# Layer 1's prompt attention: two heads' score matmuls issued in turn on the two row halves of the array

## The chip, the cores and the metric

The kernel runs on one core of a Trainium2 chip. The metric is the device time of one execution in microseconds (us). Before the change it was 2068.98 us, the median of 3 runs (2065.84 to 2069.39).

TensorE multiplies: weights are loaded into the array, a second operand streams past them, and the result lands in PSUM, which has 8 banks of 512 fp32 columns. VectorE (DVE) and ScalarE (ACT) read it from there, GpSimd (POOL) works on SBUF alone, and SyncE (SP) issues the DMAs. Each engine runs its own instructions in order and waits on semaphores for the others.

## The reference, cut to what matters

The program is one step of a 2-layer decoder for a prompt of 512 tokens and 8 samples of 8 tokens. What is changed is the prompt's part of layer 1's attention. There are 8 heads of 64 dimensions and three key groups of window and dilation (128, 1), (512, 4) and (2048, 16). Each query attends to distances 0, d, 2d, ... up to its window in each group, and the groups are merged by their softmax denominators:

```
for gi, (window, dilation) in enumerate(((128, 1), (512, 4), (2048, 16))):
    s = einsum(q[gi], k[gi]) * 64 ** -0.5, masked to distances 0, d, ..., window
    m, p = max(s), exp(s - max(s));  den = sum(p);  num = p @ v[gi]
w = exp(m - max over groups of m)
o = sum(w * num) / sum(w * den)
```

The kernel puts the scores of all three groups side by side, takes one maximum and one softmax over them, and multiplies with the values of all groups. That is the same sum.

## The kernel before, in words

Activations stand transposed: 128 channels on the partitions, tokens along the free dimension. A head pair (hp, 0 to 3) holds two heads of 64 channels, so head 0 of a pair lies on partitions 0 to 63 and head 1 on 64 to 127 of the tiles `Q[g, hp]` and `K[g, hp]`. A matmul that contracts over one head's 64 channels uses one half of the array's rows.

`layer1` runs a scheduler (`sched`, L802) over several generators. The *filler* (`fill`, L2227) issues the dense projections to q and k, head pair after head pair, and then the memory keys and values of the next stage. Three *lanes* run beside it: `win_prompt` for token residues r = 0 and r = 1, and `win_sample` for the samples' cached keys. Each goes through the four head pairs in turn and starts a head pair when its q and k are done. Every `yield` of a lane is a place where the scheduler may take another lane or the filler. With a meter (`_Meter`, L468) it keeps an estimate of when each engine is free and when each tile is written, and takes a lane up again when its last results should be there. The meter charges a TensorE matmul to the 32-column groups that its output partitions cover (L583 to L588); which rows of the array it uses does not count. All this is decided when the program is built; the chip runs the resulting fixed order.

`win_prompt` (L2279) does, for each of the two query blocks i = 0 and 1: the scores (L2288 to L2315), the exponentials, the division by the sums, transposes of the probabilities, and the product with the values. A block has 128 queries. In block 0 the scores of a head are one bank of 384 columns: a 128x256 matmul (output rows x columns) for the undilated keys, and four 64x64 ones, two groups times two residues c, whose outputs go to partition half c. In block 1 there are two banks: 128x384 for the undilated keys, and four 64x128. After each bank a `tensor_tensor_reduce` (L2310) adds the mask, writes the result to SBUF and takes the row maximum, on from the bank before. After a head's last bank a `tensor_scalar` makes -1/8 of that maximum for the exponential. The heads are done one after the other, with a `yield` after each.

All are fp32 matmuls; such a matmul shows in the trace as two records of a weight load and two of a matmul, one pair for each of its passes. The large projections are split into fp32r parts and show one record each.

Of the kernel before, what the change touches and what calls it, by code (L numbers as in the profile page):

```python
# [12 lines left out]
OP = mybir.AluOpType  # L13
# [688 lines left out]
class _Prog:  # L702
# [1576 lines left out]
    def win_prompt(self, hp, r, done, Q, K, V, O, masks, part, fin, busy):  # L2279

        nc = self.nc
        yield 0, 0, lambda: hp in done
        for i in range(2):
            yield 0, 0, lambda: not busy or self.room() >= WROOM
            busy.add(r)
            P, tt = {}, []
            qs = slice(256 * i + 128 * r, 256 * i + 128 * r + 128)
            for hh in range(2):  # L2288
                e = slice(64 * hh, 64 * hh + 64)
                mx = self.T([128, 4], "wmx")  # L2290
                den = self.T([128, 4], "wden")
                pt = []
                segs = [masks[0][r][:, 0:384], masks[1][:]] if i else [masks[0][r][:, 128:512]]
                for b, mk in enumerate(segs):
                    w = 256 if b else 384
                    ps = self.PS()
                    if b == 0:
                        k = slice(128 * i, 256 * i + 256)
                        nc.tensor.matmul(ps[:, 0:w - 128 * (1 - i)], Q[0, hp][e, qs], K[0, hp][e, k], start=True, stop=True)
                    if b == i:  # L2300
                        n = 64 + 64 * i
                        for g in range(2):
                            o = (w - 2 * n) + n * g
                            for c in range(2):
                                q0, k0 = qs.start + 64 * c, 256 * c + 128 * r
                                nc.tensor.matmul(ps[64 * c:64 * c + 64, o:o + n], Q[g + 1, hp][e, q0:q0 + 64],
                                                 K[g + 1, hp][e, k0:k0 + n], start=True, stop=True)
                    p_ = self.S([128, w], s="wP")
                    pt.append(p_)
                    nc.vector.tensor_tensor_reduce(p_[:], ps[:, :w], mk, 1.0,  # L2310
                                                   -3.0e38 if b == 0 else mx[:, 0:1], OP.add, OP.max, mx[:, b:b + 1])
                nc.vector.tensor_scalar(mx[:, 2:3], mx[:, len(segs) - 1:len(segs)], -0.125, None, op0=OP.mult)
                P[hh] = pt
                tt.append((mx, den))
                yield 1.3 if i else 0.8, 0.3 if hh == 0 else 1.5  # L2315
            nb = len(segs)
            for hh, (mx, den) in enumerate(tt):
                for b in range(nb):
                    nc.scalar.activation(P[hh][b][:], P[hh][b][:], AF.Exp, bias=mx[:, 2:3], scale=0.125,
                                         accum_out=den[:, b:b + 1])  # L2320
                yield 0, 0.2 if hh == 0 else 1.2
            for hh, (mx, den) in enumerate(tt):
                if nb == 2:
                    nc.vector.tensor_tensor(den[:, 0:1], den[:, 0:1], den[:, 1:2], op=OP.add)
                nc.vector.reciprocal(den[:, 3:4], den[:, 0:1])
                for b in range(nb):
                    nc.vector.tensor_scalar(P[hh][b][:], P[hh][b][:], den[:, 3:4], None, op0=OP.mult)
                yield 0, 0.1 if hh == 0 else 1.0
            del pt, p_
            T = {}  # L2330
            for hh in range(2):
                T[hh] = []
                for b in range(nb):
                    p_ = P[hh].pop(0)
                    ps = self.PS()
                    cuts = [128] * (2 if b else 3) if i else [128, 128, 64, 64]
                    o = 0
                    for j, w in enumerate(cuts):
                        nc.tensor.transpose(ps[:w, j * 128:j * 128 + 128], p_[:, o:o + w], self.ident)
                        o += w  # L2340
                    t = self.S([128, 128 * len(cuts)], s="wPT")
                    m = 128 * len(cuts) if i else 256
                    nc.scalar.copy(t[:, :m], ps[:, :m])
                    if i == 0:
                        nc.vector.tensor_copy(t[:64, 256:512], ps[:64, 256:512])
                    T[hh] += [_Cols(t, j * 128) for j in range(len(cuts))]
                    del p_, t
                yield 1.1 if i else 0.86, 0.2 if hh == 0 else 1.2
            po = self.PS()
            n1 = 2 + i  # L2350
            for j in range(n1 + 2):
                for hh in range(2):
                    h = 2 * hp + hh
                    o = po[64 * hh:64 * hh + 64]
                    if j < n1:
                        nc.tensor.matmul(o[:, 0:128], V[0, i + j][:, h * 64:h * 64 + 64], T[hh][j][:, 0:128],
                                         start=j == 0, stop=False)
                        continue
                    k = slice(0, 64 + 64 * i)
                    for c in range(2):  # L2360
                        x = slice(64 * c, 64 * c + 64)
                        nc.tensor.matmul(o[:, x], V[j - n1 + 1, 2 * c + r][k, h * 64:h * 64 + 64], T[hh][j][k, x],
                                         start=False, stop=j == n1 + 1 and c == 1)
            T.clear()
            busy.discard(r)
            o = O[hp][:, 256 * i:256 * i + 256].rearrange("p (n b r) -> p r b n", b=2, r=2)[:, r]
            nc.scalar.copy(o, po[:, 0:128].rearrange("p (b n) -> p b n", b=2))
            yield 1.7 if i else 1.3, 0
        part(hp, "p", r)
        if (hp, "p", 1 - r) in fin:  # L2370
            for g in range(3):
                del Q[g, hp], K[g, hp]
# [128 lines left out]
```

## Time and profile before

| | |
|---|---|
| median of 3 runs | 2068.98 us |
| profiled execution | 2069.16 us, span 2067.4 us |
| TensorE matmul, weight load | 2010.5 us (97%), 1860.1 us (90%) |
| VectorE, ScalarE, GpSimd | 1259.5 us (61%), 801.3 us (39%), 264.6 us (13%) |
| mean granted TensorE clock | 0.989 |
| the changed code | about 1117 to 1403 us of the span |

Matmul records overlap, and a record is longer than the time until the next one may start, so lengths are read here from start to start. In a merged row the shape is that of its first record: "64*128 64x256 ... x6" is two passes of a 64x256 matmul and the first four records of the 64x64 ones. "64*128" is rows times columns of the array, "64x256" the streamed operand's partitions and columns.

### The profile page before, as it was taken

How to read it: one execution, taken by the hardware profiler on the slowest of the kernel's cores; microseconds unless marked ns; L12 is line 12 of the kernel's file. 1: busy time of each engine (PE TensorE's matmuls, PEld its weight loads, DVE VectorE, ACT ScalarE, POOL GpSimd, SP SyncE). 2: the span in 40 equal slices, each digit the busy share in tenths (PEclk: the TensorE clock that was granted, in tenths of full speed). 3: DMA queues.
4: the chain of work that ended last, by engine and by line, in shares of the span. 5: the costliest groups of instructions: out<-in, count | busy, mean ns of one | idle time of the engine just before them, and what ended most of it. 6: DMA issues, size and time to landing. Idle time of an engine off the chain costs nothing.

```text
span 2067.4 us, 40636 instructions
## 1 busy us (share of the span) xinstructions
PE 2010.5 (97%) x16443; PEld 1860.1 (90%) x16443; DVE 1259.5 (61%) x3020; ACT 801.3 (39%) x1674; POOL 264.6 (13%) x570
## 2 busy tenths in 40 slices
PE   7999999999999999999999999999999999999997
PEld 6999867978999999999898878878879999999996
DVE  7785676643677377377426666655645675575575
ACT  5554434333444244144322342344434443343342
POOL 1142120000012012020003212200000021121111
PEclk9999999999999999999999999999999999999998
DMA  4222145555222222222555555566453222222222
GB/s 150 69 65 73 54 123 190 189 184 186 79 83 82 82 82 82 83 83 88 156 185 169 181 178 194 182 205 199 168 190 113 79 82 86 85 86 83 82 70 77
DMA packets 104092, 252.30 MB, mean 122 GB/s; under 512 B 11169, under 2 KB 22049, under 8 KB 103905
## 3 DMA queue, kind: packets, MB, share of 16 engines
q1 hardware_dynamic: 103760, 249.49, 37.1%
q8 instruction: 129, 2.11, 0.4%
q14 instruction: 59, 0.48, 0.1%
q10 hardware_dynamic: 144, 0.22, 0.0%
HBM read 227.70 MB, written 21.96 MB: 121 GB/s over the span
## 4 chain that ended last, share of the span: by engine, by line
PE 87%; DVE 6%; DMA 3%; ACT 3%; issue 1%; POOL 0%; SPq 0%; DVEq 0%; ACTq 0%; POOLq 0%
PE p L630 87%; DVE page L630 4%; ACT page L630 2%; DMA wr<-in_w 1%; DVE wl L630 1%; ACT wh L630 1%; DMA page<-in_cmk 1%; DVE rn L630 1%; DMA out_o_ss<-page 0%; DMA page<-xd 0%; DMA page<-in_x 0%; POOL page L630 0%; SPq L630 0%; DMA xd<-page 0%; DVE ot L630 0%
## 5 line engine op out<-in xcount | busy, mean ns | idle before, releaser
L630 PE MATMUL p<-page,wh 128*128 128x256 f32 (+1 forms) x7296 | 1103.1, 299 | 17.6 <-ACT wh L630 12.8
L630 PEld LDWEIGHTS p<-page,wh 128*128 128x128 f32 x7296 | 1012.9, 191 | 45.9 <-issue 20.6
L630 PE MATMUL p<-page,wl 128*128 128x256 f32 (+1 forms) x3648 | 589.7, 298 | 0.0
L630 PEld LDWEIGHTS p<-page,wl 128*128 128x128 f32 x3648 | 519.7, 191 | 14.0 <-issue 13.1
L630 DVE TENSOR_TENSOR page<-p,page 128x256 f32<-128x256 f32 (+5 forms) x647 | 242.1, 392 | 320.0 <-PE p L630 233.2
L630 ACT CAST wh<-wr 128x1024 fp32r<-128x1024 f32 (+1 forms) x268 | 275.6, 1031 | 391.9 <-PE p L630 313.6
L630 DVE TENSOR_TENSOR wl<-wr,wh 128x1024 fp32r<-128x1024 f32 (+1 forms) x268 | 332.9, 1245 | 83.5 <-ACT wh L630 76.7
L630 DVE SCALAR_TENSOR_TENSOR page<-page,vecs,page 128x256 f32<-128x256 f32 (+4 forms) x545 | 283.9, 526 | 97.7 <-ACT page L630 86.8
L630 PE MATMUL p<-page,page 64*64 64x64 f32 (+12 forms) x3778 | 296.7, 298 | 11.5 <-DVE page L630 4.0
L630 PEld LDWEIGHTS p<-page,page 128*32 128x32 f32 (+6 forms) x3778 | 191.1, 130 | 80.1 <-issue 30.4
L630 ACT ACTIVATE page<-page,vecs 128x256 f32<-128x256 f32 (+5 forms) x319 | 169.1, 539 | 229.7 <-DVE page L630 223.7
L630 POOL COPY page<-page 128x16 f32<-128x16 f32 (+5 forms) x312 | 128.6, 438 | 731.2 <-DVE page L630 731.2
L630 ACT ACTIVATE page<-page 128x256 f32<-128x256 f32 (+6 forms) x293 | 116.2, 412 | 139.0 <-DVE page L630 132.7
L630 POOL TENSOR_TENSOR page<-page,page 128x256 f32<-128x256 f32 (+6 forms) x93 | 90.1, 976 | 463.1 <-DVE page L630 325.9
L630 ACT COPY page<-p 128x256 f32<-128x256 f32 (+8 forms) x161 | 63.9, 413 | 186.2 <-PE p L630 185.3
L630 PE MATMUL p<-wh,page 128*128 128x512 f32 (+1 forms) x368 | 119.1, 397 | 0.0
L630 DVE TENSOR_TENSOR page<-page,page 128x256 fp32r<-128x256 f32 (+8 forms) x178 | 80.1, 462 | 57.8 <-ACT page L630 56.8
L630 DVE TENSOR_TENSOR page<-page 128x256 f32<-128x256 f32 (+5 forms) x225 | 99.4, 454 | 16.3 <-POOL page L630 11.1
L630 ACT CAST page<-page 128x256 fp32r<-128x256 f32 (+2 forms) x118 | 50.4, 442 | 125.7 <-DVE page L630 125.7
L630 PEld LDWEIGHTS p<-wh,page 128*128 128x128 f32 (+1 forms) x368 | 77.3, 223 | 14.4 <-issue 2.5
L630 PE MATMUL p<-cid,page 128*128 128x128 f32 (+3 forms) x669 | 79.4, 258 | 5.7 <-ACT page L630 4.0
L630 POOL MEMSET page<- 128x2 f32 (+4 forms) x110 | 12.2, 112 | 539.2 <-PE p L630 290.1
(84 smaller groups left out, 827.5 us busy)
## 6 DMA issues: line engine op xcount, KB each, us to landing
wr<-in_w SPq DMA_DIRECT2D x252, 512.0 KB, 3.6
page<-in_ck SPq DMA_DIRECT2D x72, 256.0 KB, 4.6
page<-in_cv SPq DMA_DIRECT2D x72, 256.0 KB, 4.2
page<-in_cmk SPq DMA_DIRECT2D x64, 256.0 KB, 5.2
page<-in_cmv SPq DMA_DIRECT2D x64, 256.0 KB, 4.9
wr<-in_w SPq DMA_DIRECT2D x16, 384.0 KB, 3.1
xd<-page SPq DMA_DIRECT2D x16, 288.0 KB, 4.3
out_o_v<-page SPq DMA_DIRECT2D x12, 256.0 KB, 4.3
```

The costliest lines, as they stand in the source:

```text
L630: return f(*args, **kw)
```

## The change

For each bank, the score matmuls of both heads are now issued in turn, into one PSUM bank for each head; the two reductions follow. The loop over banks is outermost, and the `yield` stands after each bank (in block 1 there are two) and no longer after each head. The two -1/8 scalings follow after the last `yield`. Masks, operands, counts and sizes of all instructions are as before.

```diff
             P, tt = {}, []
             qs = slice(256 * i + 128 * r, 256 * i + 128 * r + 128)
+            segs = [masks[0][r][:, 0:384], masks[1][:]] if i else [masks[0][r][:, 128:512]]
+            nb = len(segs)
             for hh in range(2):
-                e = slice(64 * hh, 64 * hh + 64)
-                mx = self.T([128, 4], "wmx")
-                den = self.T([128, 4], "wden")
-                pt = []
-                segs = [masks[0][r][:, 0:384], masks[1][:]] if i else [masks[0][r][:, 128:512]]
-                for b, mk in enumerate(segs):
-                    w = 256 if b else 384
-                    ps = self.PS()
-                    if b == 0:
-                        k = slice(128 * i, 256 * i + 256)
+                tt.append((self.T([128, 4], "wmx"), self.T([128, 4], "wden")))
+                P[hh] = []
+            for b, mk in enumerate(segs):
+                w = 256 if b else 384
+
+                pss = [self.PS() for _ in range(2)]
+                rows = [slice(64 * hh, 64 * hh + 64) for hh in range(2)]
+                if b == 0:
+                    k = slice(128 * i, 256 * i + 256)
+                    for ps, e in zip(pss, rows):
                         nc.tensor.matmul(ps[:, 0:w - 128 * (1 - i)], Q[0, hp][e, qs], K[0, hp][e, k], start=True, stop=True)
-                    if b == i:
-                        n = 64 + 64 * i
-                        for g in range(2):
-                            o = (w - 2 * n) + n * g
-                            for c in range(2):
-                                q0, k0 = qs.start + 64 * c, 256 * c + 128 * r
+                if b == i:
+                    n = 64 + 64 * i
+                    for g in range(2):
+                        o = (w - 2 * n) + n * g
+                        for c in range(2):
+                            q0, k0 = qs.start + 64 * c, 256 * c + 128 * r
+                            for ps, e in zip(pss, rows):
                                 nc.tensor.matmul(ps[64 * c:64 * c + 64, o:o + n], Q[g + 1, hp][e, q0:q0 + 64],
                                                  K[g + 1, hp][e, k0:k0 + n], start=True, stop=True)
+                for hh, ps in enumerate(pss):
+                    mx = tt[hh][0]
                     p_ = self.S([128, w], s="wP")
-                    pt.append(p_)
+                    P[hh].append(p_)
                     nc.vector.tensor_tensor_reduce(p_[:], ps[:, :w], mk, 1.0,
                                                    -3.0e38 if b == 0 else mx[:, 0:1], OP.add, OP.max, mx[:, b:b + 1])
-                nc.vector.tensor_scalar(mx[:, 2:3], mx[:, len(segs) - 1:len(segs)], -0.125, None, op0=OP.mult)
-                P[hh] = pt
-                tt.append((mx, den))
-                yield 1.3 if i else 0.8, 0.3 if hh == 0 else 1.5
-            nb = len(segs)
+                del pss, ps
+                yield 1.3, 0.3 if b < nb - 1 else 1.5
+            for mx, den in tt:
+                nc.vector.tensor_scalar(mx[:, 2:3], mx[:, nb - 1:nb], -0.125, None, op0=OP.mult)
```

On TensorE, at block 0 of the first head pair, the kernel before has head 0's set into one bank (p_11760) and then head 1's into the next (p_11770), lane 0:

```order
L630 MATMUL p_11760<-page_11409,page_11338 128x256
L630 MATMUL p_11760<-page_4141,page_11409 64x64 x2
L630 MATMUL p_11760<-page_4141 64x64 x2
L630 MATMUL p_11770<-page_11409,page_11338 128x256
L630 MATMUL p_11770<-page_4141,page_11409 64x64 x2
L630 MATMUL p_11770<-page_4141 64x64 x2
L630 MATMUL p_11788<-page_11009,page_10800 32x512 x2
L630 MATMUL p_11788<-page_6120,page_10800 32x512
L630 MATMUL p_11788<-page_11009,page_10800 32x512
```

The same place on TensorE after the change, where p_11762 is head 0's bank and p_11763 head 1's, and p_11780 begins lane 1's block 0:

```order
L630 MATMUL p_11762<-page_11409,page_11338 128x256
L630 MATMUL p_11763<-page_11409,page_11338 128x256
L630 MATMUL p_11762<-page_4141,page_11409 64x64
L630 MATMUL p_11763<-page_4141,page_11409 64x64
L630 MATMUL p_11762<-page_4141,page_11409 64x64
L630 MATMUL p_11763<-page_4141,page_11409 64x64
L630 MATMUL p_11762<-page_4141 64x64
L630 MATMUL p_11763<-page_4141 64x64
L630 MATMUL p_11762<-page_4141 64x64
L630 MATMUL p_11763<-page_4141 64x64
L630 MATMUL p_11780<-page_11409,page_11338 128x256
L630 MATMUL p_11781<-page_11409,page_11338 128x256
```

The heads alternate from matmul to matmul, and lane 1's pair, which stood behind a sample's four 32x512 and two dense matmuls, now follows at once.

On TensorE at block 1 of the first head pair, the kernel after the change has both lanes' 128x384 matmuls in a row, each into a bank of its own, then lane 0's 64x128:

```order
L630 MATMUL p_11989<-page_11409,page_11338 128x384
L630 MATMUL p_11990<-page_11409,page_11338 128x384
L630 MATMUL p_11999<-page_11409,page_11338 128x384
L630 MATMUL p_12000<-page_11409,page_11338 128x384
L630 MATMUL p_12005<-page_4141,page_11409 64x128
L630 MATMUL p_12006<-page_4141,page_11409 64x128
L630 MATMUL p_12005<-page_4141,page_11409 64x128
L630 MATMUL p_12006<-page_4141,page_11409 64x128
L630 MATMUL p_12005<-page_4141 64x128
L630 MATMUL p_12006<-page_4141 64x128
L630 MATMUL p_12005<-page_4141 64x128
L630 MATMUL p_12006<-page_4141 64x128
```

Lane 1's 64x128 follow after sixteen 32x128 matmuls of the sample. Before, each head had its 128x384 and its four 64x128 together, and other work of the lanes and the filler stood between some of the heads.

On VectorE, at block 0 of the first head pair, the kernel after the change issues these; each ISA row with a p_ operand is one mask-and-maximum reduction, the ISA row behind it reads its maximum out, and the TENSOR_SCALAR rows are the -1/8 scalings:

```order
L630 ISA page_11367,wmx_11758<-p_11762,page_6120 128x384
L630 ISA wmx_11758 128x1
L630 ISA page_11367,wmx_11760<-p_11763,page_6120 128x384
L630 ISA wmx_11760 128x1
L630 ISA page_11367,wmx_11776<-p_11780,page_6120 128x384
L630 ISA wmx_11776 128x1
L630 ISA page_11367,wmx_11778<-p_11781,page_6120 128x384
L630 ISA wmx_11778 128x1
L630 TENSOR_SCALAR wmx_11758<-wmx_11758 128x1
L630 TENSOR_SCALAR wmx_11760<-wmx_11760 128x1
```

Before, each reduction's scaling stood right behind it, and a sample's reduction stood between those of lane 0 and lane 1.

## Rows read from the trace of the kernel before

**Rows 1.** The page, part 1: busy us, share of the span, instructions.

```profile
PE 2010.5 (97%) x16443; PEld 1860.1 (90%) x16443; DVE 1259.5 (61%) x3020; ACT 801.3 (39%) x1674; POOL 264.6 (13%) x570
```

**Rows 2.** The chain in order of time: start us, us, what.

```profile
1132.05 72.36 PE p L630 x796
...
1205.87 73.08 PE p L630 x802
...
1279.68 58.05 PE p L630 x648
...
1339.62 54.59 PE p L630 x631
```

**Rows 3.** Stretches of layer 1's attention.

```profile
core 0: us, PE busy (x) PEld busy (x) DVE busy (x) ACT busy (x) POOL busy (x), PEclk, DMA share, GB/s
1180.00:1340.00 160.00, 157.59 (x1685) 132.31 (x1683) 102.67 (x293) 57.70 (x149) 37.95 (x52) 1.00 0.58 191
1340.00:1350.00 10.00, 10.00 (x52) 5.53 (x51) 6.22 (x18) 2.97 (x9) 0.00 (x0) 0.55 0.22 59
1350.00:1400.00 50.00, 50.00 (x634) 39.81 (x635) 29.91 (x89) 24.75 (x67) 0.00 (x0) 0.99 0.65 212
```

**Rows 4.** Waits of TensorE, 1117 to 1403: us in total, times, longest.

```profile
PE p L630 <- DVE page L630: 2.5, 4, 1.1
PE p L630 <- ACT page L630: 0.4, 1, 0.4
```

**Rows 5.** TensorE in time, block 0, head pair 0: start us, us, what, records.

```profile
1117.87 0.96 PE L630 MATMUL p<-page,page 64*128 64x256 f32 x6
1118.66 0.28 PE L630 MATMUL p<-page 64*64 64x64 f32 x4
1118.88 0.96 PE L630 MATMUL p<-page,page 64*128 64x256 f32 x6
...
1119.88 1.07 PE L630 MATMUL p<-page,page 128*32 128x512 f32 x8
```

**Rows 6.** TensorE in time, block 1, head pair 0.

```profile
1139.01 1.27 PE L630 MATMUL p<-page,page 64*128 64x384 f32 x6
...
1140.44 1.27 PE L630 MATMUL p<-page,page 64*128 64x384 f32 x6
...
1141.86 0.55 PE L630 MATMUL p<-cid,page 128*128 128x128 f32 x3
...
1143.22 1.27 PE L630 MATMUL p<-page,page 64*128 64x384 f32 x6
```

**Rows 7.** TensorE in time, block 0, head pair 3; idle time and its releaser in brackets.

```profile
1338.10 0.38 PE L630 MATMUL p<-page,wh 128*128 128x256 f32 x1 [0.38 <-ACT page L630]
1339.62 3.08 PE L630 MATMUL p<-page,wh 128*128 128x256 f32 x13 [1.14 <-DVE page L630]
1342.63 1.63 PE L630 MATMUL p<-page,page 64*128 64x256 f32 x6
...
1347.94 1.93 PE L630 MATMUL p<-page,page 128*32 128x512 f32 x8
...
1350.95 1.07 PE L630 MATMUL p<-page,page 64*128 64x256 f32 x6
...
1352.07 1.06 PE L630 MATMUL p<-page,page 128*32 128x512 f32 x8
```

**Rows 8.** TensorE in short stretches, inside a set of each kind.

```profile
1118.50 0.33 PE L630 MATMUL p<-page,page 64*64 64x64 f32 x4
...
1135.33 0.59 PE L630 MATMUL p<-page,page 64*128 64x384 f32 x1
...
1136.17 0.43 PE L630 MATMUL p<-page,page 64*64 64x128 f32 x4
```

**Rows 9.** TensorE in layer 0: alone, alone, together, and short stretches of the last.

```profile
252.29 1.16 PE L630 MATMUL p<-page,page 64*128 64x128 f32 x8
...
257.96 1.12 PE L630 MATMUL p<-page,page 64*128 64x512 f32 x2
...
260.57 1.35 PE L630 MATMUL p<-page,page 64*128 64x512 f32 x10
...
260.57 0.79 PE L630 MATMUL p<-page,page 64*128 64x512 f32 x4
...
261.11 0.59 PE L630 MATMUL p<-page,page 64*128 64x512 f32 x4
```

**Rows 10.** VectorE's groups, 1117 to 1403: count, busy us, mean ns, idle before.

```profile
L630 DVE CUSTOM_DVE_ANT_0 page<-p,page 128x384 f32<-128x384 f32 x32 | 17.8, 556 | 20.5 <-PE p L630 20.4
...
L630 DVE CUSTOM_DVE_ANT_0 page<-p,page,wmx 128x256 f32<-128x256 f32 x16 | 7.7, 484 | 2.3
...
L630 DVE DVE_READ_ACCUMULATOR2_ANT wmx<- 128x1 f32 x48 | 4.0, 83 | 0.0
```

**Rows 11.** TensorE in time: transposes after block 0, a sample's 32 records.

```profile
1127.92 0.60 PE L630 MATMUL p<-cid,page 128*128 128x128 f32 x4
...
1309.44 1.08 PE L630 MATMUL p<-page,page 128*32 128x128 f32 x32
```

**Rows 12.** TensorE in time, the output projection's first weights.

```profile
1409.97 0.50 PE L630 MATMUL p<-wl,page 128*128 128x512 f32 x1 [1.45 <-DVE wl L630]
```

More of the change, by code (lines that the diff above doesn't have):

```diff
@@ L2328, in win_prompt @@
                 yield 0, 0.1 if hh == 0 else 1.0
-            del pt, p_
+            del p_
             T = {}
```

## The prediction

> **What bounds the kernel now.** I read the page first, then the chain in order of time, the stretches of layer 1's attention, the matmuls inside them, and the waits. On the page TensorE is busy for 97% of the span [rows 1]. That share alone proves little, since matmul records overlap; the chain is what tells. Through this attention it is TensorE almost without a break: three pieces of 72.36, 73.08 and 58.05 us, then 54.59 us [rows 2]. The stretches agree: TensorE has 157.59 of 160 us at full clock (1.00, that is 2.4 GHz), VectorE only 102.67 [rows 3]. And what TensorE waits for from 1117 to 1403 us is 2.9 us in all [rows 4]. So a microsecond of array time saved here comes off the end, unless a new wait takes it.
>
> **What a score set costs.** The changed code runs 4 head pairs x 2 lanes (r) x 2 query blocks (i) x 2 heads = 32 score sets. An fp32 matmul leaves two records, one for each pass. A set of block 0 is one 64x256 matmul and four of 64x64; it starts at 1117.87, the next at 1118.88, the sample's work at 1119.88: 1.005 us each [rows 5]. A set of block 1 is one 64x384 and four of 64x128: 1139.01, 1140.44, 1141.86, so 1.425 us [rows 6]. These rows stand for 12 and 16 sets, alike to some ns. In the last head pair three sets of block 0 fell into a stretch of granted clock 0.55, which is mostly the lower level of 1.2 GHz: 1342.63 to 1347.94, 5.31 us, and the fourth took 1.12 [rows 7]. All 32 together: 12 x 1.005 + 5.31 + 1.12 + 16 x 1.425 = 41.3 us. Counted at full clock, as I do below, they are 16 x 1.005 + 16 x 1.425 = 38.9 us.
>
> Where do the 1.005 us go? The two kinds of set differ in the first matmul by 128 columns. Its two passes take 0.63 us (1117.87 to the first 64x64 at 1118.50) against 0.84 us (1135.33 to the first 64x128 at 1136.17) [rows 5, 8], so 128 columns cost 0.105 us a pass. 256 columns then stream in 2 x 0.21 = 0.42 us and not in 0.63; the other 0.2 us go into entering the 64-row layout and leaving it. At the same rate the eight 64x64 passes would need 8 x 0.053 = 0.42 us alone; they take 0.38 with the way out, so they run two by two on the array's column halves, in four steps, 0.21 us. So some 0.37 us of a set are layout changes and 0.63 us streaming.
>
> **What two row halves do together.** One place shows it. In layer 0 a 64x512 matmul of the sample tokens (rows 0 to 63, all columns) meets the eight records of a scan step's second half chunk (rows 64 to 127, all columns; it is the fourth group of eight, and the scan takes lower and upper half chunks in turn). Alone, the two 64x512 records span 1.12 us and the eight of 64x128 span 1.16; together all ten span 1.35 us [rows 9]. One after the other they would need some 2 us. So the halves stream side by side, in the same columns and into two banks, which is the case here.
>
> **The change part by part.**
> *The scores.* Nothing is added or removed in arithmetic: the same matmuls, reductions, exponentials and DMAs. Each pair of sets becomes one alternating run. If the halves overlap, a pair takes as long as one set plus the second head's offset at issue; I take 0.03 us: 8 x 1.035 + 8 x 1.455 = 19.9 us. That saves 38.9 - 19.9 = 19.0 us.
> *The order.* For block 0 both lanes' pairs now stand next to each other with nothing between. For block 1 the four 64x384 of both lanes come first, then lane 0's 64x128, the sample's matmuls, lane 1's 64x128. Before, block 1 went back and forth between 64x384 and 64x128 for each head and entered the layout from outside three times a head pair (1135.33, 1139.01, 1143.22 [rows 6, 8]). I book 0.7 us in all for that, about 0.2 a head pair; ends 0 and 1.5 (one change of 0.37 each).
> *Loading the weights.* No row shows two row halves loading weights of the same columns at the same moment. If these loads queue, the 64x64 steps of block 0 double, 8 x 0.21 = 1.7 us, and each of the 16 pairs begins later by one load, at most the 0.1 us of a 128-column pass, 1.6 us more: ends 0 and -3.3. The overlap in [rows 9] lost almost nothing, so I take -1.0.
> *VectorE and ScalarE.* A pair's two 128x384 reductions (0.556 us and a read of 0.083; 0.484 for 256 columns [rows 10]) now come due together, where the first used to run beside the second head's matmuls. The delay is about 0.65 us a pair. It is hidden by what follows on TensorE: for block 0 the other lane's pair, a sample set (1.07 us, the 128x512 records [rows 5]) and dense work. From lane 0's scores (done 1119.88) to its transposes (1127.92) lie 8 us before the change [rows 5, 11], and the new order puts twenty dense matmuls more between them in the first head pair. The two -1/8 scalings move behind the reductions and cost nothing while that cover stands. The planner still charges the two heads' matmuls one after the other, so it believes TensorE later than it is by about what a pair saves (1.0 or 1.4 us), and places the next steps that much too early. Block 1 is tightest: eight reductions in a row need 4 x 0.64 + 4 x 0.57 = 4.8 us, during which their banks are held. The bank that lane 1's 64x128 takes frees after the second reduction, 0.84 + 1.28 = 2.1 us from the first score; TensorE gets there after two 64x384 pairs (0.84 + 0.63), one run of 64x128 (1.425 - 0.84 = 0.58) and the sample's 32 records (1.08 [rows 11]), at about 3.1. Ends: 0, and a full exposed pair of reductions each time, 16 x 1.28 = 20 us. The waits shown are 2.9 us over the whole stage, so I take 1.5 us more.
> *DMA.* The sample's cache loads and the weights keep their number and have some 6% less time; TensorE shows no DMA wait there [rows 4], and the share is 0.65 at its highest here [rows 3]. No cost taken.
> *After the stage.* TensorE is the bound again [rows 1], and the start of everything later moves with it. The output projection's first weights make TensorE wait 1.45 us [rows 12]; that may move by as much either way.
>
> Sum: 19.0 + 0.7 - 1.0 - 1.5 = 17.2 us gained. The profiled execution is 2069.16 us (span 2067.4 and 1.8 around it), so 2052.0; it stands 0.18 above the median of 2068.98, so against that 2051.8.
>
> **The rivals.**
> 1. *Passes keep their written order.* Then a matmul's first pass runs only beside the last pass of the one before: 64x256 pairs need three slots instead of two (+0.21), the 64x64 nine slots instead of four (+0.27): 1.52 us for block 0, and 1.455 + 0.32 + 5 x 0.105 = 2.30 for block 1. Saved: 8 x (2.01 - 1.52) + 8 x (2.85 - 2.30) = 8.3 us, less 1 of waits: 2062. Against it: the 64x512's second pass starts at 261.11, and by 261.10 three passes of the 64x128, written after it, have begun [rows 9]. Chance 5%. The Trainium skill, "TensorE: Matmul & The Clock Gate", Part 3 on packing, says that matmuls start and end strictly in program order; by that rule this rival would be the forecast, 2062. The trace disagrees for fp32 on different row halves: three passes overtook.
> 2. *The halves do not overlap here.* Perhaps because four tiles work at once. Only layout changes are saved, 16 x 0.37 = 5.9 us: 2063. Again [rows 9] speaks against it. 4%.
> 3. *The wait moves to VectorE.* Half to all of the 20 us of reductions becomes visible: 2060 to 2070, 2064 taken. For it: a VectorE that is 64% busy over these stretches [rows 3] and more behind the scores, and a planner that misjudges TensorE. Against: the 2.9 us of waits, the dense work placed behind the scores. 6%. The Trainium skill, "TensorEngine Tiling (Array Packing)", Gotcha 1, warns that row tiling raises the pressure on PSUM; that is this rival's way.
> 4. *The clock falls: slower.* Where TensorE ran dry for 0.38 and 1.14 us near 1339 us, the clock then granted was the lower one for some 10 us, and three sets took 5.31 us instead of 3.02 [rows 7]. If the faster score blocks leave TensorE dry in the same way, each such stretch costs about 5 us, half of its ten. There are 8 places (two blocks, four head pairs); 17.2 / 5 says that from the fourth on the gain is gone, and with six it is 2051.8 + 30 = 2082. Against it: sample sets and dense matmuls stand behind every block. 4%.
>
> **How the numbers follow.** Forecast 81%, rivals 5, 4, 6 and 4%. Within the forecast the unknowns are -3.3 to 0 for loads, 0 to 6 for waits, and one slow-clock stretch more or less (5 us): 2044 to 2061. To leave out no more than 2 in 10 the range takes in rival 1's 2062: 2044.5 to 2062. A measurement of this kernel tells 0.2%, 4.1 us, from no change. Faster by more than that: the forecast, rivals 1 and 2, half of rival 3: 0.92. Same: 0.04. Slower: 0.04.
>
> **What would show it.** In the changed profile a pair of block 0 should span about 1.0 us from its first 64x256 to the next lane's, with starts of the two heads some ns apart; block 1's four 64x384 some 1.4 to 1.5 us. The sum of all score runs should be near 20 us. TensorE's waits from VectorE in the stage should stay under 6 us, and the stage end about 17 us earlier, with nothing lost behind it. Pairs of 1.5 us mean rival 1, of 1.65 us rival 2. Wrong altogether would be pairs of 2 us, or a granted clock under 1 in several stretches before 1330 us.

## The result, and the profile after

The changed kernel takes **2044.39 us** (median of 4 runs, 2042.96 to 2046.02) against 2067.41 for the kernel before on the same chip (median of 4; a fourth run of 2062.36 joined the three that gave 2068.98): ratio 0.9889, 95% interval 0.9874 to 0.9905. That is 23.0 us where 17.2 were forecast, and 0.11 us below the low end of the range. The 0.11 alone says little: two of the four runs lie inside the range, and on another chip the same kernel's median is 2045.26. The mechanism is the predicted one; the size of the gain is not.

TensorE is still the bound. Page, part 1, of the changed kernel (busy us, share of the span, instructions), which answers to [rows 1]:

```profile
PE 1987.4 (97%) x16443; PEld 1849.4 (91%) x16443; DVE 1252.5 (61%) x3020; ACT 798.2 (39%) x1674; POOL 264.2 (13%) x570
```

The same instructions, 23 us less of TensorE. Its chain of waits from 1050 us on (start us, us, what; the first piece is cut at 1050), which answers to [rows 2]:

```profile
1049.99 271.07 PE p L630 x2818
...
1322.95 9.10 PE p L630 x79
...
1341.27 19.49 PE p L630 x289
```

The breaks ahead of and between the pieces of 72.36, 73.08 and 58.05 us of before are gone. The last head pair, from 1322.95, is now more broken than it was.

Block 0, head pair 0, TensorE in time (start us, us, what, records), which answers to [rows 5]:

```profile
1117.60 0.98 PE L630 MATMUL p<-page,page 64*128 64x256 f32 x12
1118.40 0.30 PE L630 MATMUL p<-page 64*64 64x64 f32 x8
1118.62 0.98 PE L630 MATMUL p<-page,page 64*128 64x256 f32 x12
1119.42 0.30 PE L630 MATMUL p<-page 64*64 64x64 f32 x8
1119.65 1.07 PE L630 MATMUL p<-page,page 128*32 128x512 f32 x8
```

A row of x12 and the x8 behind it are now both heads of one lane, 20 records instead of 10. Two pairs take 1119.65 - 1117.60 = 2.05 us, 1.024 each; one set alone took 1.005. The second head costs 0.02 us.

Block 1, two short stretches, which answer to [rows 6]:

```profile
1133.42 1.94 PE L630 MATMUL p<-page,page 64*128 64x384 f32 x16
```

```profile
1135.18 0.40 PE L630 MATMUL p<-page 64*64 64x128 f32 x8
1135.51 0.32 PE L630 MATMUL p<-page,page 128*32 128x128 f32 x4
```

The four 64x384 of both lanes and lane 0's pair of 64x128 end at 1135.51, 2.09 us after they began; lane 1's pair of 64x128, behind the sample, is 0.60 more (1136.52 to 1137.12). So block 1 of a head pair takes 2.69 us instead of 4 x 1.425 = 5.70, and all the score runs at full clock 8 x 1.024 + 4 x 2.69 = 18.9 us instead of 38.9.

Waits of TensorE in the changed kernel, 1117 to 1381 us (us in total, times, longest), which answer to [rows 4]:

```profile
PE p L630 <- DVE page L630: 2.5, 2, 1.4
PE p L630 <- ACT page L630: 1.4, 2, 1.0
```

The total rose from 2.9 to 3.9 us, but the waits are others. In the kernel before, three of VectorE's four waits stood ahead of block 1's sample work, as in this row:

```profile
1132.05 1.08 PE L630 MATMUL p<-page,page 128*32 128x128 f32 x32 [0.44 <-DVE page L630]
```

Of these three (1.3 us up to 1300 us) the changed kernel has none: it shows no wait at all in head pairs 0 to 2. All of its waits lie around the last one, which answers to [rows 7]:

```profile
1321.42 0.38 PE L630 MATMUL p<-page,wh 128*128 128x256 f32 x1 [0.37 <-ACT page L630]
1322.95 3.18 PE L630 MATMUL p<-page,wh 128*128 128x256 f32 x13 [1.15 <-DVE page L630]
1326.06 3.49 PE L630 MATMUL p<-page,page 64*128 64x256 f32 x48
1329.48 0.51 PE L630 MATMUL p<-page,wh 128*128 128x256 f32 x2
...
1341.27 3.17 PE L630 MATMUL p<-page,page 128*32 128x128 f32 x60 [1.39 <-DVE page L630]
...
1366.10 2.34 PE L630 MATMUL p<-page,page 128*64 128x128 f32 x58 [0.98 <-ACT page L630]
```

The first two waits were there before, 0.38 and 1.14; those at 1341.27 and 1366.10 are new. The stretches (columns as in [rows 3]):

```profile
1180.00:1320.00 140.00, 140.00 (x1632) 120.30 (x1631) 92.11 (x276) 53.76 (x142) 34.38 (x46) 1.00 0.61 203
1320.00:1330.00 10.00, 8.48 (x74) 5.83 (x73) 8.73 (x24) 5.39 (x13) 1.56 (x3) 0.83 0.57 193
```

TensorE is busy for all of the 140 us, at full clock. Behind the idle place the clock fell as before, but for less long: a PEclk of 0.83 over 10 us is 3.4 us at the lower level, where before it was 0.55 over ten [rows 3].

So where did the time go? The span fell by 25.0 us (2067.4 to 2042.4). From start to start of the same instruction in the two traces:

| stretch | before | after | difference |
|---|---|---|---|
| up to the first score run | 1117.87 | 1117.60 | -0.3 |
| head pairs 0 to 2, to the first scores of pair 3 | 224.76 | 208.46 | -16.3 |
| head pair 3, to the first 128x512 of the output projection | 60.03 | 54.72 | -5.3 |
| from there to the end | 664.71 | 661.61 | -3.1 |

### The profile page after: what moved, and what is told of

The parts are those of the page before. It is cut to its first block, busy times and chain, and to the rows that moved or that the text cites. A ratio compares the mean times of both kernels' runs of the same rounds, so it can differ in the third digit from the quotient of the medians.

```text
span 2042.4 us, 40671 instructions
## 1 busy us (share of the span) xinstructions
PE 1987.4 (97%) x16443; PEld 1849.4 (91%) x16443; DVE 1252.5 (61%) x3020; ACT 798.2 (39%) x1674; POOL 264.2 (13%) x570
## 4 chain that ended last, share of the span: by engine, by line
PE 87%; DVE 6%; ACT 3%; DMA 3%; issue 1%; POOL 0%; SPq 0%; DVEq 0%; ACTq 0%; POOLq 0%
PE p L630 87%; DVE page L630 4%; ACT page L630 2%; DVE wl L630 1%; DMA wr<-in_w 1%; ACT wh L630 1%; DVE rn L630 1%; DMA page<-in_cmk 1%; DMA out_o_ss<-page 0%; DMA page<-xd 0%; DMA page<-in_x 0%; POOL page L630 0%; ACT L630 0%; SPq L630 0%; DMA xd<-page 0%
## 5 line engine op out<-in xcount | busy, mean ns | idle before, releaser
L630 PE MATMUL p<-page,page 64*64 64x64 f32 (+13 forms) x3768 | 280.7, 297 | 10.6 <-DVE page L630 4.0
L630 PEld LDWEIGHTS p<-page,page 64*64 64x64 f32 (+6 forms) x3768 | 184.0, 130 | 69.5 <-issue 20.7
L630 POOL TENSOR_TENSOR page<-page,page 128x320 f32<-128x320 f32 (+6 forms) x96 | 91.7, 963 | 446.1 <-DVE page L630 321.8
```

What stands on the lines that cost most here:

```text
L630: return f(*args, **kw)
```

## The experiments

Each is told by its edit on the kernel before or the changed one. "Head pair" times are from its first score run to the next pair's: 73.80 us before and 68.36 after for pairs 0 and 1, which all profiles of the two kernels repeat to 0.02 us.

**Is it the alternation, or the new order around it?** *grouped* leaves all else where the changed kernel has it, and issues a bank's matmuls head by head. *byshape* sorts them by tile shape first and then by head.

```
+ mms.append((hh, 0 or 1, (out, Q, K)))        # 1: the 64x64 or 64x128
+ for m in mms: self.meter.note("tensor", "matmul", m[2], {})   # planner: as changed
+ for m in sorted(mms, key=lambda m: m[0]):    # byshape: (m[1], m[0])
+     self.tc.nc.tensor.matmul(*m[2], start=True, stop=True)
```

> The changed kernel with only the order inside a bank pair undone: head 0's score matmuls of a bank first, then head 1's. Everything else (banks, reductions, planned order of all other work) stays as in the changed kernel. Theory (row halves overlap when their matmuls are neighbours): in block 0 head 0's 64x64 need another layout than its 64x256, so head 1 comes wholly behind and a pair takes 2.0 us again instead of 1.02: 8 us more. In block 1 the 64x384 of the heads are still neighbours and stay at 1.49 us for four; the 64x128 of head 1 stand behind four of head 0, and take 0.60 or up to 1.1 us a pair: 0 to 4 us more. In all 2052 to 2057. Rival (the gain came from the new order of the lanes' steps): no more than 1 us over the changed kernel, 2044 to 2046.

> The changed kernel with the matmuls of a bank pair grouped by layout: both heads' large matmuls, then head 0's four small ones, then head 1's four. Theory A (a row half runs ahead of the other by several matmuls): as the changed kernel, 2044 to 2045, 64x64 of a pair still 0.39 us. Theory B (only the next matmul or two can run beside): block 0's small ones take 0.6 instead of 0.39, block 1's 1.05 instead of 0.60: 8 x 0.2 + 8 x 0.45 = 5 us more, 2049.

*grouped*: 2057.11 us (median of 12), ratio to before 0.9968 (0.9953 to 0.9982), 0.11 above the 2052 to 2057 that were expected. *byshape*: 2044.54 us (median of 6), ratio 0.9904 (0.9887 to 0.9920): as the changed kernel. Block 0 of *grouped* in head pair 1, TensorE in time:

```profile
1189.73 0.96 PE L2315 MATMUL p<-page,page 64*128 64x256 f32 x6
1190.52 0.28 PE L2315 MATMUL p<-page 64*64 64x64 f32 x4
1190.73 0.96 PE L2315 MATMUL p<-page,page 64*128 64x256 f32 x6
```

A set takes 1190.73 - 1189.73 = 1.00 us, as before: the first head's 64x64 and the second head's 64x256 use different row halves and yet do not overlap. In *byshape* they do:

```profile
1114.07 0.99 PE L2315 MATMUL p<-page,page 64*128 64x256 f32 x12
1114.87 0.31 PE L2315 MATMUL p<-page 64*64 64x64 f32 x8
1115.11 0.99 PE L2315 MATMUL p<-page,page 64*128 64x256 f32 x12
```

1.04 us a pair, though here four 64x64 of the first head stand ahead of the second head's four. So matmuls of one tile shape overlapped in both orders tried, and neighbours of the two shapes 64x64 and 64x128 (rows x columns of the array) did not. Block 1 overlaps in *grouped* too, since there a bank holds one shape at a time:

```profile
1207.53 1.95 PE L2315 MATMUL p<-page,page 64*128 64x384 f32 x16
1209.29 0.41 PE L2315 MATMUL p<-page 64*64 64x128 f32 x8
1209.63 1.08 PE L630 MATMUL p<-page,page 128*32 128x128 f32 x32
```

These are 2.10 us, as in the changed kernel, and the head pair of 70.35 us (1189.73 to 1260.08) bears it out: of the 5.44 us a head pair that the change saves, 1.99 hang on having the two heads' matmuls of one shape next to each other in block 0, and 3.45 (the old wait of 0.44 included) come with the same in block 1.

**The kernel before once more**, for a second look at its slow-clock stretch.

> The kernel before, a second profile. If the slow-clock stretch at the fourth head pair is of one length whatever happens (10.24 us from 1341 on), it comes out the same and so does the time, 2067 to 2069. If its length changes from run to run, it is 3.4 or 6.8 us in some, and the time is then 1.7 to 3.4 us shorter.

One run, 2071.4 us. Head pairs of 73.82 and 73.80 us again; the lower clock in the last head pair began at 1339.7 and lasted 17.1 us (10.2 in the first profile), and that head pair took 62.74 us up to the output projection instead of 60.03. The 20 us in question:

```profile
1337.00:1357.00 20.00, 18.49 (x116) 10.80 (x115) 12.54 (x36) 6.91 (x17) 1.24 (x2) 0.57 0.40 140
```

**What does that stretch cost?** *busy_before* and *busy_after* put eight matmuls, whose result nobody reads, into the idle place ahead of the last head pair of either kernel.

```
+ ps = self.PS()
+ for _ in range(8):
+     self.tc.nc.tensor.matmul(ps[:, 0:256], self.ident, m0[0][:, 0:256], start=True, stop=True)
  yield from self.mem_kv(1)
```

> The kernel before with eight fp32 128x256 matmuls of the identity into a bank that nobody reads, on TensorE between the last q and k projection and the first memory key projection, where it stood idle for some 3 us before 1341. Theory (that idle time brings the slow clock, and the slow stretch costs half its length): no slow stretch there, head pair 3's block 0 sets at 1.005 us; 4 to 5 us gained there less up to 0.5 for matmuls that do not fit into the idle time: 2062 to 2064. Rival (the clock falls for another reason, or costs nothing): 3.4 us of matmuls partly added, 2068 to 2071.

> The changed kernel plus the same eight filler matmuls at the idle place ahead of the last head pair. Theory (the change is worth about 20.5 us of array work at full clock, and the rest of its gain is a shorter slow-clock stretch in the last head pair): no stretch of lower clock between 1300 and 1400 us, and a time of 2041.5 to 2044, that is 19 to 21.5 us below the kernel before with the same filler (2062.95). Rival (the clock has no part in the gain): the two kernels with filler differ by the same 23 us as those without, 2040.

*busy_before*: 2062.95 us (median of 12), ratio 0.9987 (0.9977 to 0.9998), as expected of a clock that stays up. (The idle time there is 0.38 and 1.14 us [rows 7], 1.5 and not the 3 of the expectation.) *busy_after*, on another chip: 2045.45 us (median of 4), ratio 0.9908 (0.9891 to 0.9925), above both expectations; there is no gain to be seen. Since the two stood on different chips, both ran again on one chip, beside the kernels without the filler (*filler_before*, *filler_after*, *after_third*).

> The changed kernel, so that all four of these stand on one chip beside the kernel before. 21 to 25 us below the kernel before, as first measured (ratio 0.988 to 0.990); head pairs of 68.35 us; in the last head pair waits of TensorE of 1.4 (from VectorE) and 0.9 to 1.0 us (from ScalarE).

> The kernel before with the filler matmuls, again, on the chip of the others. Theory (the slow-clock stretch behind the idle place costs the kernel before more than the changed one): 2 to 7 us below the kernel before, ratio 0.9965 to 0.999. Rival (the clock explains none of the prediction's shortfall): within 1 us of the kernel before.

> The changed kernel with the filler matmuls, again. Theory: with the clock at its upper level in both, the change is worth what was summed for the array, 16 to 18.5 us between this one and the kernel before with filler (ratio of the two 0.991 to 0.9925), and this kernel is within 2 us of the changed one. Rival: 21 to 25 us lie between the two with filler as well.

| same chip | median | ratio to before |
|---|---|---|
| before (17 runs) | 2065.86 | |
| after_third (6) | 2045.26 | 0.9896 (0.9878 to 0.9914) |
| filler_before (12) | 2062.73 | 0.9981 (0.9971 to 0.9992) |
| filler_after (5) | 2043.68 | 0.9891 (0.9873 to 0.9908) |

The change alone is at 20.6 us here, a little under what was expected. The filler is worth 3.1 us to the kernel before (its interval excludes 1) and 1.6 to the changed one, whose runs with and without it overlap. With filler the change is worth 19.05 us: between the two expectations, and nearer to the theory, whose 16 to 18.5 was still too low. The difference between 3.1 and 1.6 is within the scatter of the runs. The mean granted clock of each run is another way to separate the two: over the 17 runs of before, the time falls from 2073.73 us in the run at 0.986 to 2063.79 and 2063.98 in the two at 0.993. Among runs at 0.992 the kernel before has a median of 2064.31 (5 runs) and *after_third* of 2044.50 (4 runs): 19.8 us at an equal clock. *filler_before*, TensorE in time and its clock:

```profile
1337.51 3.62 PE L2239 MATMUL p<-page,cid 128*128 128x256 f32 x16
1340.78 2.02 PE L630 MATMUL p<-page,wh 128*128 128x256 f32 x14
1342.72 0.96 PE L630 MATMUL p<-page,page 64*128 64x256 f32 x6
1343.52 0.28 PE L630 MATMUL p<-page 64*64 64x64 f32 x4
1343.73 0.96 PE L630 MATMUL p<-page,page 64*128 64x256 f32 x6
```

```profile
1335.00:1350.00 15.00, 15.00 (x114) 11.05 (x113) 11.37 (x32) 7.01 (x18) 3.01 (x5) 1.00 0.62 210
```

No idle place, the clock at 1.00, and a score set of 1.00 us again where it was 1.77 [rows 7]. The filler itself gains no time (1263.43 to 1340.69, 77.26 us, for the third head pair in *busy_before*; 77.15 without): it only takes the place of the waits. From the last head pair's scores to the output projection it is 56.26 us in both profiles with filler, 60.03 and 62.74 without. In the changed kernel the same stretch is 54.21 and 54.55 with, 54.56 to 54.80 without.

**A second profile of the changed kernel.**

> The changed kernel once more, for a second profile. Theory (the array's work is fixed, the length of the slow-clock stretches is not): from the first score run of one head pair to that of the next 68.35 us to within 0.05 for the first three, as before; the lower clock in the last head pair again begins right behind the idle place but may last anything from 3.4 to 10.2 us; span 2041 to 2046.

2043.46 us, span 2041.3. Head pairs of 68.35 and 68.36; the third, with the idle place in it, 71.76 (the expectation overlooked that place). The lower clock lasted 3.4 us in this profile and in *after_third*'s as in the first. So 3 of 3 profiles have the short stretch, and 2 of 2 of the kernel before a longer one.

**Whose fault are the new waits in the last head pair?** *aware* tells the planner that the two row halves of a score run work side by side.

```
+ half = self.halves and k <= 0.5 and op != "transpose"
+ g = self.groups[e0:e0 + 1] if half else self.groups   # busy until, by row half and column group
+ self.meter.halves = True      # around the score matmuls; aware_last: hp == 3
```

> The changed kernel with a planner that charges the two row halves apart inside the score runs, so that it believes TensorE where it is. Theory (the new waits of 1.39 and 0.98 us in the last head pair come from the planner's late idea of TensorE): these two waits shrink to under 1 us together, 2041.5 to 2043.5. Rival (they come from the chain through VectorE and ScalarE itself, which has nothing left to hide behind in the last head pair): same waits, 2044 to 2045.5. In the first three head pairs both expect 68.3 us each, as now.

> Both edits together: the planner that charges the row halves apart, and the eight filler matmuls. If each does what its theory says: 2039.5 to 2042, the fastest of all. If the planner's idea of TensorE does not matter: as the changed kernel with filler alone, 2041.5 to 2044.

*aware*: 2045.48 us (median of 4), ratio 0.9908 (0.9893 to 0.9923), not better. Its waits did shrink; of the 2.37 us this is left:

```profile
1344.51 1.31 PE L635 MATMUL p<-page,page 128*64 128x128 f32 x22 [0.49 <-ACT page L635]
```

But head pairs 0 and 1 rose to 69.07 and 68.96 us, which neither side expected: the planner now keeps the two lanes' 64x384 apart, and the array enters their layout twice. And the lower clock behind the idle place lasted 6.8 us from 1326.1 in this profile, against 3.4 in the changed kernel's:

```profile
1326.00:1333.00 7.00, 7.00 (x56) 3.48 (x55) 5.18 (x16) 1.31 (x4) 0.00 (x0) 0.51 0.24 77
```

So the last head pair took 54.00 us up to the output projection here, and 51.58 in *aware_busy*, where the clock stayed up. *aware_busy*: 2042.55 us (median of 4), ratio 0.9891 (0.9876 to 0.9906), above its theory's range and in the other side's. The better version was to use the edit in the last head pair alone:

> The changed kernel with the planner that charges the row halves apart in the last head pair alone, so that the first three keep their order. If the waits in the last head pair come from the planner's late idea of TensorE, as the kernel with it in all head pairs suggested (one wait of 0.49 us left of 2.37): 1.5 to 2.5 us below the changed kernel, and head pairs 0 to 2 at 68.35 us and not 69.0. If the gain there came from the other order further up: as the changed kernel, and the waits of 1.4 and 0.9 us are there again.

*aware_last*: **2041.70 us** (median of 5, 2038.83 to 2042.24), ratio 0.9875 (0.9858 to 0.9893); every run lies below every one of *after_third*'s on the same chip (2043.57 to 2048.50). Head pairs 0 and 1 are at 68.35 and 68.36, and where TensorE waited 1.39 us there is no gap:

```profile
1338.73 0.66 PE L635 MATMUL p<-cid,page 128*128 128x128 f32 x4
1339.32 3.17 PE L635 MATMUL p<-page,page 128*32 128x128 f32 x60
```

From the last pair's scores to the output projection it is 52.17 us instead of 54.56 to 54.80. It beats both kernels.

## Why the prediction fell short

The mechanism, the bound and the sign held; the sum left about 6 us out. Three of its terms failed: the slow-clock stretch and what follows the stage, both put at nothing, and the loads, which wrongly took 1.0 us off. Term by term, with "full clock" from the profiles with filler:

| term | predicted | measured |
|---|---|---|
| scores and their order | 19.0 + 0.7 | 38.9 - 18.9 = 20.0 |
| loads of weights | -1.0 | none seen |
| waits in the stage | -1.5 | about -1.8 |
| slow-clock stretch | 0 | 1 to 3.5 |
| after the stage | 0 | about 2 |

**Scores: right.** A pair of block 0 takes 1.024 us (predicted 1.035). Block 1 takes 10.8 us in all against 11.6 less the 0.7 of order.

**Loads: wrong, by 1.0 us.** I took -1.0 because no row showed two row halves loading at once. The pair's 0.02 us over a single set leaves no room for it, with four 64x64 tiles at work.

**Waits: right in sum, for other reasons.** Head pairs 0 to 2 gained the three old waits, 1.3 us. Their stretch shrank by 16.3 us = 3 x 4.98 of scores + 1.3. The last pair at full clock went only from 56.26 to 54.4 us, 1.9 where its scores gave 5.0: the new waits took 2.2 to 2.6 of it and some 0.7 is not assigned. The cover that I named, dense work behind the scores, had not run out: in the changed kernel dense matmuls follow both waits (the second wait is at 1366.10).

```profile
1348.49 0.73 PE L630 MATMUL p<-page,wh 128*128 128x256 f32 x4
...
1368.68 0.96 PE L630 MATMUL p<-page,wh 128*128 128x256 f32 x6
```

The order left the waits open. *grouped*, with the same planned order, has them too (1.39 and 1.12 us) although there only block 1 overlaps. That the planner believes TensorE late was named as a cause; in *aware_last*, where it is told of the overlap, both waits are gone and the last head pair is 2.4 to 2.6 us shorter (52.17 against 54.56 to 54.80). The 3.6 us between the medians (2045.26 to 2041.70) are more than that, and the rest is not assigned.

**Slow clock: the first step that failed.** I saw that three sets took 5.31 us instead of 3.02 at the lower clock [rows 7], wrote "counted at full clock, as I do below", and took "one slow-clock stretch more or less" into the range as if either sign were as likely. But the profiled execution, against which the sum was made, contained one such stretch, in the very code that changes, and the changed kernel's stretch there is a third as long (3.4 us, not 10.2). The stretch cost 3.8 us (60.03 to 56.26) in that profile, 6.5 in the second (62.74), and 0.2 to 0.4 in the changed kernel's (54.56 to 54.80 against 54.4). So about 3.5 us of the gain is the clock between the two profiles that were compared. By medians it is less: 3.1 less 1.6, that is 1.5 us, with the filler, and 20.6 less 19.8, about 1, at equal clock. That execution of 2069.16 us was itself a slow draw: later medians of the kernel before are 2065.86 (17 runs) and 2065.90 (23 runs). Measured by the 19.8 us at equal clock, some 3 of the first chip's 23.0 us are the clock and the chance of four runs. The other 2.6 above the forecast are of the size of the two remaining misses: 1.0 of loads and about 2 after the stage.

**After the stage: the second step that failed.** From the output projection's first matmul to the last matmul of the kernel it is 655.0 to 656.4 us in four profiles before and 653.1 to 654.6 in five after: about 2 us by their means, part of the gain that I booked at 0 with 1.45 either way. The wait on weights of [rows 12] shrank:

```profile
1397.92 0.50 PE L630 MATMUL p<-wl,page 128*128 128x512 f32 x1 [0.41 <-DVE wl L630]
...
1431.27 1.13 PE L630 MATMUL p<-page,cid 128*128 128x256 f32 x4 [1.04 <-DVE page L630]
```

The 1.45 is now 0.41, and three more of about 0.25 are gone; 1.04 of VectorE, which was 0.63, takes some back. The waits on these weights come to 2.2 to 2.7 us in the four profiles before and to 0.4 to 0.9 in the five after. A further 1.0 us between the two profiles that were compared is a wait on the load of the memory keys (us in total, times, longest; before, then after):

```profile
PE p L630 <- DMA page<-in_cmk: 1.9, 2, 1.3
```

```profile
PE p L630 <- DMA page<-in_cmk: 0.9, 1, 0.9
```

This one comes and goes: the second profile before has 0.9 too. No experiment was made on this term alone, and why these waits shrank stays open.

Rival 1 (written order) and rival 2 (no overlap) fall by the pairs of 1.02 us; rival 1 also by *byshape*, where by strict order the two heads' 64x64 could not have run side by side. The Trainium skill says in "TensorE: Matmul & The Clock Gate", Part 3, that matmuls start strictly in program order; *byshape* disagrees with that for fp32 matmuls on two row halves. Rival 3 is true in the last head pair alone, at 2.2 to 2.6 us (waits for VectorE and ScalarE together) of its 20. Rival 4 went the other way: one slow-clock stretch, not four, and a shorter one.

Open is why the stretch at the lower clock lasts 3.4 us in the changed kernel, 6.8 in *aware*, and 10.2 or 17.1 in the kernel before, with the same idle place ahead of it.

## What to carry to other kernels

The fp32 score matmuls on the two row halves of the array overlapped almost wholly when neighbours in program order had the same tile shape (1.024 us a pair for 1.005 a set); with 64x64 and 64x128 tiles in turn they did not (2.0 us), so look at the shapes before the alternation. When a sum is made against a profiled execution, ask which clock each stretch had there and whether the changed kernel will have the same: the stretch of 60.03 us took 56.26 with the clock up, a difference that no term for the array's work covers. And compare that execution with more runs, since one at a low mean clock makes the gain look larger. A planner that was not told of the overlap left waits in the last head pair alone, and telling it paid only there (2041.70 us, against 2045.48 when it was told everywhere).

## What the runs showed of the hardware

- Two score sets of block 0 on the two row halves took 1.024 us against 1.005 for one, with four 64x64 tiles at work at once in their second part (0.39 us for both heads' 64x64, 1118.23 to 1118.62, against 0.38 for one head's).
- A row half ran ahead of matmuls written before: with four 64x64 of one head ahead of the other's four (*byshape*), a pair took 1.04 us instead of 1.02. Engines were introduced as running their instructions in order; TensorE's matmuls did not begin in the written order here.
- 64x64 tiles on one row half and a 64x128 tile on the other did not overlap at all: 1.00 us a set in *grouped*.
- The lower clock also came without an idle place: in *grouped* TensorE was busy for all 12 us up to 1120, and from 1119.7 the clock was at 1.2 GHz for 6.8 us, during the fourth of four unpaired sets in a row; that head pair took 73.37 us where the next took 70.35. In its head pairs 1 and 2 the same four sets kept the full clock, so this is seen, not explained:

```profile
1108.00:1120.00 12.00, 12.00 (x93) 10.33 (x91) 7.66 (x20) 2.10 (x2) 4.75 (x6) 0.99 0.74 256
1120.00:1126.00 6.00, 6.00 (x33) 3.54 (x36) 2.19 (x13) 3.90 (x9) 0.08 (x1) 0.50 0.56 200
```
